# Hybrid decoder layer: q left unnormalised up to the exponential, both norm gains on k, masked copies for two heads

## Chip, cores and metric

One core of one Trainium2 chip. The metric is the device time of one launch in microseconds (us); for the kernel before, three runs gave 1914.89, 1916.03 and 1916.34, median 1916.03. The profile is of one execution.

## The reference

One layer over a sequence of 2048 tokens of width 1024, float32. The attention part is what the change touches:

```python
h = rms_norm(x, attn_norm_g);  z = h @ w_in          # columns: q, k, v, and three conv groups
q = rms_norm(z[..., :512].reshape(b, s, 8, 64), q_norm_g)     # 8 heads of 64
k = rms_norm(z[..., 512:640].reshape(b, s, 2, 64), k_norm_g)  # 2 kv heads
v = z[..., 640:768].reshape(b, s, 2, 64)
# blocks of 128 queries see their own block of keys and the one before
sc = einsum('bnqhgd,bnkhd->bnhgqk', q, k) * 64 ** -0.5
sc = where(0 <= query - key < 128 and key >= 0, sc, -1e30)
p = softmax(concatenate([sc, sink], -1))[..., :-1]   # one learned sink for each head
y_attn = einsum('bnhgqk,bnkhd->bnqhgd', p, v)
x = x + concatenate([rms_norm(y_attn, attn_out_g), rms_norm(y_conv, conv_out_g)]) @ w_out
x = x + square(relu(rms_norm(x, mlp_norm_g) @ w_up)) @ w_down
```

## The kernel before

A product in float32 is made of three products of rounded parts: every operand is split into a high and a low part (ACT rounds the high part, DVE subtracts it to get the low one), and TensorE adds high x high, high x low and low x high into one PSUM bank (`mm3`, L278 to L280).

The mixer stage, which the change touches, goes through four chunks of 512 tokens, each of four blocks of 128 (blocks b0 to b15). After it come the two MLP stages, products of `w_up` (L1454) and of `w_down` (L1571), which the change does not touch.

In a chunk, `mixers` runs the attention of the blocks one after another and weaves other work of the chunk between its steps (`fill`): the three convolution products (`pc`, `px`, `pb`), the output projection (`pout`), the transposes of the next chunk's input (`pt_a`) and its q, k, v projection (`pz`). The attention of a block has these steps:

- `qk_norm`: ACT squares q and k (L679), DVE sums over each of the 10 heads (L681), GpSimd raises the mean to the power -0.5 (L192, L193) into `rq`, 128 x 10, of which there are two buffers. DVE multiplies q and k by it (L684) and then by the gains (L686, once for the 512 columns of q and once for the 128 of k), in place in `z`.
- `qk_transpose`: TensorE transposes q (L697) and k (L699) into PSUM; ACT and DVE split them into `qt` and `kw` (L702 to L709).
- `softmax`: for each of four pairs of heads TensorE makes the scores against both key blocks (L724), ACT copies the own block's scores to `sc` (L732), and DVE overwrites those later than the query with the scores of the block before (L735), one head at a time. In block 0 there is none before, and a constant -1e30 is written. Then DVE takes the maximum of each row, negated (L737), limits it by the sink (L738), ACT makes eight exponentials with that as bias, each with its row sum (L741), and one of the sinks (L746); DVE adds the sink to the sums, takes the reciprocal and multiplies (L747 to L749).
- `values`: TensorE transposes the probabilities (L760), ACT and DVE split them (L766, L767), GpSimd keeps the part that lies in the own block (L773, into `pp` tiles with three buffers), and TensorE multiplies with v (L812).

PSUM has eight banks: three with the tag `mm` for projections, four with the tag `at` for attention, and one, `tr`, for the transposes of inputs, all handed out in turn. A scheduler fixes the order on each engine when the kernel is built: by the program's order, by its own estimates of durations, and by the offsets of `PRIO` (through `ahead(i)`) and the counts of `FILL`. Both tables stay as they are. On the chip every engine then takes its instructions in that order and waits where a semaphore asks for it. Loads go out in order on SP.

At the start, g_qk holds the two gains, 64 columns each, for all partitions; the gain of q is multiplied by 64 ** -0.5 (L1104), and the sinks are negated into `nsink` (L1107).

Of the kernel before, what the change touches and what calls it, by code (L numbers as in the profile page):

```python
# [11 lines left out]
AF = mybir.ActivationFunctionType  # L12
ALU = mybir.AluOpType
# [3 lines left out]
P = 128  # L17
# [3 lines left out]
HEADS, KVH, DH = 8, 2, 64  # L21
# [14 lines left out]
NT = CH // P  # L36
# [68 lines left out]
def hymba_layer(  # L105
# [19 lines left out]
    nc = tc.nc  # L125
# [37 lines left out]
    def zrow(name):  # L163
# [13 lines left out]
    later = const.tile([P, P], I32, name="later")  # L177
    nc.gpsimd.memset(later, 1)
    nc.gpsimd.affine_select(
        later, later, pattern=[[1, P]], compare_op=ALU.is_gt, fill=0.0, base=0, channel_multiplier=-1  # L180
    )
    neg = const.tile([P, 1], F32, name="neg")
# [305 lines left out]
    g_qk = const.tile([P, 2, DH], F32, name="g_qk")  # L488
# [144 lines left out]
    with tc.tile_pool(name="first", bufs=1) as first:  # L633
        with tc.manual_schedule(engines={ET.PE, ET.Activation, ET.DVE, ET.Pool, ET.SP}):
            rs0_in = first_chunk(first)

    with tc.tile_pool(name="mix_small", bufs=1) as mix_small, tc.tile_pool(name="mix", bufs=1) as mix:
# [10 lines left out]
        def project_qkv(c, h, z):  # L648

            z += [zrow(f"z{c}_{t}") for t in range(NT)]  # L650
            both = [[by_k(w) for w in weights(None, c, f"q{half}")] for half in range(2)]
            w4 = [w.rearrange("p (k c) -> p k c", k=KD) for w in weights(None, c, "qkv2")]

            for pc, t in ((0, 0), (0, 1), (1, 0), (0, 2), (0, 3), (1, 1), (1, 2), (1, 3)):
                n = 256 if pc else AW
                ps = bank("mm", f"pz{c}_{pc}_{t}")[:, :n]
                hk = lambda s, k, t=t: h[s][:, k, t * P : (t + 1) * P]
                wk = (lambda s, k: w4[s][:, k, :]) if pc else (lambda s, k: both[k // (KD // 2)][s][:, k % (KD // 2), :])
                for k in range(KD):
                    mm3(ps, lambda s, k=k: hk(s, k), lambda s, k=k: wk(s, k), k == 0, k == KD - 1)  # L660
                    if (k % 2 or not pc) and k < KD - 1:
                        yield
                nc.scalar.copy(z[t][:, pc * AW : pc * AW + n], ps)
                if pc and not t:
                    qk_norm(c * NT, z[0])
                yield


# [1 line left out]
            nc.gpsimd.memset(row("xt", f"xt_first{i}", 2)[:, :1], 0.0)  # L670

        nh = HEADS + KVH
        mix_small.tile([P, 8], F32, name="mix_pad")

        def qk_norm(b, zt):
            nm = f"b{b}"
            zqk = zt[:, : nh * DH].rearrange("p (h d) -> p h d", h=nh)
            sq = mix.tile([P, nh, DH], F32, tag="sq", name=f"sq_{nm}", bufs=1)
            nc.scalar.activation(sq, zqk, AF.Square, scale=DH**-0.5)  # L679
            ssq = mix_small.tile([P, nh], F32, tag="ssq", name=f"ssq_{nm}", bufs=2)  # L680
            nc.vector.tensor_reduce(ssq, sq, axis=AX.X, op=ALU.add)  # L681
            rq = mix_small.tile([P, nh], F32, tag="rq", name=f"rq_{nm}", bufs=2)
            rsqrt(rq, ssq)
            nc.vector.tensor_tensor(zqk, zqk, rq[:, :, None].to_broadcast([P, nh, DH]), op=ALU.mult)  # L684
            for i, (h0, h1) in enumerate(((0, HEADS), (HEADS, nh))):
                nc.vector.tensor_tensor(  # L686
                    zqk[:, h0:h1], zqk[:, h0:h1], g_qk[:, i, None, :].to_broadcast([P, h1 - h0, DH]), op=ALU.mult
                )
        def qk_transpose(b, zt):

            nm = f"b{b}"
# [17 lines left out]
                )  # L709
            return qt  # L710

        def softmax(b, qt):


            nm = f"b{b}"
            nk = (2 if b else 1) * P
            own = b % 2
            sc = mix.tile([P, HEADS, P], F32, tag="sc", name=f"sc_{nm}", bufs=2)
            for pr in range(HEADS // 2):
                kv = pr * 2 // GQ  # L720
                ps = bank("at", f"psc_{nm}_{pr}").rearrange("p (h s k) -> p h s k", h=2, s=2)
                for j in range(2):
                    for r in range(2):
                        nc.tensor.matmul(  # L724
                            ps[:, j].rearrange("p s k -> p (s k)")[:, :nk],
                            qt[:, pr, j, :],
                            kw[:, r, kv, :, :].rearrange("p s k -> p (s k)")[:, :nk],
                            start=r == 0,
                            stop=r == 1,
                        )  # L730
                s2 = sc[:, pr * 2 : pr * 2 + 2, :]
                nc.scalar.copy(s2, ps[:, :, own, :])  # L732
                for j in range(2):
                    other = ps[:, j, 1 - own, :] if b else neg.to_broadcast([P, P])
                    nc.vector.copy_predicated(s2[:, j, :], later, other)  # L735
            ngm = mix_small.tile([P, HEADS], F32, tag="ngm", name=f"ngm_{nm}", bufs=2)
            nc.vector.tensor_reduce(ngm, sc, axis=AX.X, op=ALU.max, negate=True)  # L737
            nc.vector.tensor_tensor(ngm, ngm, nsink, op=ALU.min)  # L738
            den = mix_small.tile([P, HEADS], F32, tag="den", name=f"den_{nm}", bufs=2)
            for hd in range(HEADS):  # L740
                nc.scalar.activation(  # L741
                    sc[:, hd, :], sc[:, hd, :], AF.Exp, bias=ngm[:, hd : hd + 1], accum_out=den[:, hd : hd + 1]
                )
            es = mix_small.tile([P, HEADS], F32, tag="es", name=f"es_{nm}", bufs=2)
            nc.vector.tensor_tensor(es, sink, ngm, op=ALU.add)
            nc.scalar.activation(es, es, AF.Exp)  # L746
            nc.vector.tensor_tensor(den, den, es, op=ALU.add)  # L747
            nc.vector.reciprocal(den, den)
            nc.vector.tensor_tensor(sc, sc, den[:, :, None].to_broadcast([P, HEADS, P]), op=ALU.mult)  # L749
            return sc  # L750
# [280 lines left out]
        def mixers(c, before, h, z):  # L1031


            last = c + 1 == NCHUNK
            n_fill = FILL[c]
            stage[0] = c
            at, yt, x1, h_next, z_next = [], [], [], [], []
            ra = small.tile([P, NT], F32, tag="ra", name=f"ra{c}", bufs=2)
            rc = small.tile([P, NT], F32, tag="rc", name=f"rc{c}", bufs=2)
            steps = besides(c, before, h, yt, rc, x1, h_next, z_next)  # L1040
            left = out_projection(c, 0, at, ra, x1)

            spare = (NT - 1) * NCT if last else 0

            def fill(n):
                nonlocal spare
                for _ in range(n):
                    if next(steps, steps) is steps and spare:
                        spare -= 1
                        next(left)  # L1050

            def scores(t):
                with ahead(0):
                    qt = qk_transpose(c * NT + t, z[t])
                fill(n_fill[t + 1][0])
                with ahead(1):
                    sc = softmax(c * NT + t, qt)
                if t + 1 < NT:
                    with ahead(2):
                        qk_norm(c * NT + t + 1, z[t + 1])  # L1060
                return sc

            if not c:
                qk_norm(0, z[0])
            fill(n_fill[0][0])
            sc = [scores(0)]
            fill(n_fill[0][1])
            for t in range(NT):
                b = c * NT + t
                if t + 1 < NT:  # L1070
                    sc.append(scores(t + 1))
                fill(n_fill[t + 1][1])
                for late in range(2):
                    if t and late == ((c, t) in LATE_RSTD):
                        with ahead(3):
                            attn_rstd(b - 1, sqa, ra[:, t - 1 : t])
                    if not late:
                        fill(n_fill[t + 1][2])
                a, sqa = values(b, z[t], z[t - 1][:, O_V:O_B] if t else v_last, sc[t], n_fill[t + 1][3:], fill)
                at.append(a)  # L1080
            for _ in steps:
                pass

            def rest():
                for i, _ in enumerate(left):
                    if i == REST:
                        attn_rstd(b, sqa, ra[:, NT - 1 : NT])
                    yield

            return rest(), h_next, z_next  # L1090

        z = z0
# [7 lines left out]
        for t in range(NT):  # L1100
            nc.tensor.transpose(pr[:, t * P : (t + 1) * P], rs0_at[:, 1, t * P : (t + 1) * P], ident)
        nc.scalar.copy(rs0_row, pr)
        with tc.issue_after(rs0_in):
            nc.gpsimd.tensor_scalar(g_qk[:, 0, :], g_qk[:, 0, :], DH**-0.5, None, op0=ALU.mult)  # L1104
        nsink = const.tile([P, HEADS], F32, name="nsink")
# [9 lines left out]
        for c in range(NCHUNK):  # L1115
            left, h, z = mixers(c, left, h, z)
# [215 lines left out]
    wts, ps, vs = {}, {}, {}  # L1332
# [278 lines left out]
```

## Time and profile before

| | before |
|---|---|
| median of three runs | 1916.03 us (1914.89 to 1916.34) |
| profiled execution: span from the first to the last instruction | 1913.4 us |
| instructions | 24557 |
| mean granted TensorE clock | 1.000 |

A time by the clock of the runs contains a little before and after the span: the median lies 2.6 us above it. In the rows below, a group's row gives the line, the engine, the operation, what it writes and reads with the shapes, and how often; then busy us in all and mean ns of one; then how long the engine was idle just before it, and who ended that. A row of the timeline begins with the start in us and the duration. "PEld" is TensorE's weight load, which runs ahead of the matmuls.

### The profile page before, as it was taken

The page shows a single profiled execution, that of the slowest core. Times are in us where ns is not written, and L with a number is a line of the kernel's source. Part 1 is how long each engine was busy: PE and PEld are TensorE (multiplying, and loading weights), DVE is VectorE, ACT ScalarE, POOL GpSimd, SP SyncE. Part 2 cuts the span into 40 slices and gives each one's busy share as a digit, 9 for nine tenths or more (in the row PEclk, how much of TensorE's full clock was granted, in tenths as well). Part 3 has the DMA queues.
Part 4 walks back from the last instruction along what each step waited for, and adds up shares of the span by engine and source line. Part 5 has one row for each costly group of instructions (what it writes and reads, how often), then busy time and mean ns, then how long its engine had stood idle before and what let it go on. Part 6 is the DMA issues. An engine that isn't in the chain of part 4 may idle for free.

```text
span 1913.4 us, 24557 instructions
## 1 busy us (share of the span) xinstructions
PE 1907.7 (100%) x8930; PEld 1591.1 (83%) x8930; DVE 1202.7 (63%) x1857; ACT 829.4 (43%) x1557; POOL 274.4 (14%) x477
## 2 busy tenths in 40 slices
PE   9999999999999999999999999999999999999999
PEld 8888888888888888888888888888888888888887
DVE  5895567448467759998788766666534334457531
ACT  6564245335445346544555545453332332232320
POOL 2123212302221112233101111111000000100000
PEclk9999999999999999999999999999999999999999
DMA  9984844564578688777576544448954457766631
GB/s 305 333 320 120 329 189 177 213 227 160 203 266 277 215 294 251 221 215 244 195 233 213 175 145 159 140 148 321 364 198 150 138 171 224 281 228 213 217 124 55
DMA packets 232792, 413.80 MB, mean 216 GB/s; under 512 B 51672, under 2 KB 136416, under 8 KB 219872
## 3 DMA queue, kind: packets, MB, share of 16 engines
q1 hardware_dynamic: 203840, 336.59, 52.0%
q0 software_dynamic: 15424, 51.40, 6.9%
q10 hardware_dynamic: 13408, 24.26, 3.4%
q8 instruction: 70, 1.15, 0.2%
q14 instruction: 50, 0.41, 0.1%
HBM read 286.35 MB, written 125.83 MB: 215 GB/s over the span
## 4 chain that ended last, share of the span: by engine, by line
PE 99%; DVE 0%; POOL 0%; issue 0%; ACT 0%; DVEq 0%; POOLq 0%
PE u L1454 32%; PE d L1571 32%; PE pout L278 3%; PE pout L280 3%; PE pout L279 3%; PE pz L278 2%; PE pz L280 2%; PE pz L279 2%; PE psc_b L724 2%; PE pb_c L280 2%; PE pb_c L279 2%; PE pb_c L278 2%; PE px_c L278 2%; PE px_c L279 2%; PE px_c L280 2%; PE po_b L812 1%
## 5 line engine op out<-in xcount | busy, mean ns | idle before, releaser
L1454 PE MATMUL u<-op_x,wop 128*128 128x512 f32 x2688 | 609.7, 389 | 0.0
L1571 PE MATMUL d<-op_w,op_f 128*128 128x512 f32 x2691 | 609.5, 389 | 0.0
L1571 PEld LDWEIGHTS d<-op_w,op_f 128*128 128x128 f32 x2691 | 504.8, 188 | 104.7
L1454 PEld LDWEIGHTS u<-op_x,wop 128*128 128x128 f32 x2688 | 504.3, 188 | 105.3 <-issue 0.3
L434 DVE TENSOR_TENSOR op_f<-op_f 128x1024 fp32r<-128x1024 f32 x112 | 136.8, 1224 | 235.6 <-ACT op_f L433 235.4
L433 ACT CAST op_f<-op_f 128x1024 fp32r<-128x1024 f32 x112 | 117.7, 1051 | 349.5 <-DMA op_f<-fop 349.0
L452 ACT CAST wop<-wu 128x512 fp32r<-128x512 f32 x156 | 96.1, 619 | 92.0 <-PE u L1454 88.3
L453 DVE TENSOR_TENSOR wop<-wu,wop 128x512 fp32r<-128x512 f32 x156 | 110.2, 708 | 31.8 <-ACT wop L452 16.7
L1190 POOL DMA_DIRECT2D fop<-s x96 | 52.1, 542 | 443.2 <-DVE s L1193 436.7
L1196 DVE TENSOR_TENSOR u<-u,u 128x512 f32<-128x512 f32 x128 | 87.7, 685 | 19.4 <-PE u L1454 19.2
L434 DVE TENSOR_TENSOR op_w<-raw,op_w 128x1024 fp32r<-128x1024 f32 x56 | 68.3, 1221 | 28.8 <-ACT op_w L433 28.8
L433 ACT CAST op_w<-raw 128x1024 fp32r<-128x1024 f32 x56 | 58.8, 1052 | 48.4 <-PE d L1571 26.3
L1202 ACT ACTIVATE u<-u 128x512 f32<-128x512 f32 x64 | 40.5, 632 | 56.5 <-DVE u L1196 54.3
L741 ACT ACTIVATE sc_b<-sc_b,ngm_b 128x128 f32<-128x128 f32 x128 | 49.7, 389 | 30.0 <-DVE ngm_b L738 30.0
L773 POOL TENSOR_SCALAR_AFFINE_SELECT pp_b<-pp_b 128x512 fp32r<-128x512 f32 x60 | 41.3, 701 | 134.6 <-ACT pp_b L766 66.1
L1403 POOL DMA_DIRECT2D wds<-raw x16 | 8.5, 533 | 329.9 <-DVE raw L1401 329.9
L453 DVE TENSOR_TENSOR wop<-wu_s,wop 128x512 fp32r<-128x512 f32 x64 | 45.9, 718 | 11.9 <-ACT wop L452 11.7
L452 ACT CAST wop<-wu_s 128x512 fp32r<-128x512 f32 x64 | 39.4, 620 | 29.3 <-PE u L1454 24.9
L278 PE MATMUL pout<-w_wo,yt_c 128*128 128x512 f32 x128 | 51.5, 402 | 0.0
L280 PE MATMUL pout<-w_wo,yt_c 128*128 128x512 f32 x128 | 51.0, 398 | 0.0
L279 PE MATMUL pout<-w_wo,yt_c 128*128 128x512 f32 x128 | 50.2, 393 | 0.0
L735 DVE COPY_PREDICATED sc_b<-later,psc_b 128x128 f32<-128x128 int32 x120 | 29.4, 296 | 32.0 <-ACT sc_b L732 31.7
(265 smaller groups left out, 3119.0 us busy)
## 6 DMA issues: line engine op xcount, KB each, us to landing
op_f<-fop SPq DMA_DIRECT2D x112, 512.0 KB, 4.3
raw<-in_w_down_dram SPq DMA_DIRECT2D x72, 512.0 KB, 4.1
wu<-in_w_up_dram SPq DMA_DIRECT2D x128, 256.0 KB, 3.8
w_wo<-wo SPq DMA_DIRECT2D x24, 1024.0 KB, 6.7
fop<-s POOLq DMA_DIRECT2D x96, 256.0 KB, 2.6
fop<-u ACTq DMA_DIRECT2D x64, 256.0 KB, 2.6
op_x<-xop SPq DMA_DIRECT2D x28, 512.0 KB, 6.0
w_q<-q SPq DMA_DIRECT2D x12, 1024.0 KB, 6.7
```

The source lines that it names most:

```text
L278: nc.tensor.matmul(ps, st(0), mv(0), start=first, stop=False)
L279: nc.tensor.matmul(ps, st(0), mv(1), start=False, stop=False)
L280: last_sum[0] = nc.tensor.matmul(ps, st(1), mv(0), start=False, stop=last).ins
L433: nc.scalar.copy(op[:, 0], raw)
L434: nc.vector.tensor_tensor(op[:, 1], raw, op[:, 0].bitcast(F32), op=ALU.subtract)
L452: splits.append(nc.scalar.copy(hi, blk).ins)
L453: lows.append(nc.vector.tensor_tensor(lo, blk, hi.bitcast(F32), op=ALU.subtract).ins)
L741: nc.scalar.activation(sc[:, hd, :], sc[:, hd, :], AF.Exp, bias=ngm[:, hd : hd + 1], accum_out=den[:, hd : hd + 1])
L1190: eng.dma_start(fop_dram[tb][ORDER_DOWN.index(i)][n // 2][:, n % 2], b)
L1196: return nc.vector.tensor_tensor(dst, ps, b, op=ALU.add).ins
L1454: nc.tensor.matmul(pt, wops[i][:, a, k, :], xops[tb, p][k // 2][:, b, k % 2, :], start=p not in GOES_ON and k + j == 0, stop=k + j == NB + ...
L1571: nc.tensor.matmul(ps[tb][j][:, cs], fs[tb][:, a, k, j * P : (j + 1) * P], w[:, b, k, cs], start=first and p not in GOES_ON and k + n == 0 ...
```

## The change

Four edits:

1. `qk_norm` multiplies only k by `rq` and by a gain; q stays as it comes from the projection. `rq` is returned and handed to `softmax` (through the table `rqs`).
2. The row maximum is taken of the scores without q's factor, so it is multiplied by `rq` of the head (a new DVE instruction of 128 x 8), and the exponential gets `rq` of the head as its scale, beside the bias that it has.
3. The gain of q is multiplied into that of k, once, on GpSimd, ahead of the factor 64 ** -0.5.
4. The masked copy takes a pair of heads in one instruction, with the mask repeated over the two heads.

```diff
-                    qk_norm(c * NT, z[0])
+                    rqs[c * NT] = qk_norm(c * NT, z[0])
...
             rsqrt(rq, ssq)
-            nc.vector.tensor_tensor(zqk, zqk, rq[:, :, None].to_broadcast([P, nh, DH]), op=ALU.mult)
-            for i, (h0, h1) in enumerate(((0, HEADS), (HEADS, nh))):
-                nc.vector.tensor_tensor(
-                    zqk[:, h0:h1], zqk[:, h0:h1], g_qk[:, i, None, :].to_broadcast([P, h1 - h0, DH]), op=ALU.mult
-                )
+            zk = zqk[:, HEADS:]
+            nc.vector.tensor_tensor(zk, zk, rq[:, HEADS:, None].to_broadcast([P, KVH, DH]), op=ALU.mult)
+            nc.vector.tensor_tensor(zk, zk, g_qk[:, 0, None, :].to_broadcast([P, KVH, DH]), op=ALU.mult)
+            return rq
+
...
-        def softmax(b, qt):
+        def softmax(b, qt, rq):
...
                 nc.scalar.copy(s2, ps[:, :, own, :])
-                for j in range(2):
-                    other = ps[:, j, 1 - own, :] if b else neg.to_broadcast([P, P])
-                    nc.vector.copy_predicated(s2[:, j, :], later, other)
+                other = ps[:, :, 1 - own, :] if b else neg[:, :, None].to_broadcast([P, 2, P])
+                nc.vector.copy_predicated(s2, later[:, None, :].to_broadcast([P, 2, P]), other)
...
             nc.vector.tensor_reduce(ngm, sc, axis=AX.X, op=ALU.max, negate=True)
+            nc.vector.tensor_tensor(ngm, ngm, rq[:, :HEADS], op=ALU.mult)
             nc.vector.tensor_tensor(ngm, ngm, nsink, op=ALU.min)
...
                 nc.scalar.activation(
-                    sc[:, hd, :], sc[:, hd, :], AF.Exp, bias=ngm[:, hd : hd + 1], accum_out=den[:, hd : hd + 1]
+                    sc[:, hd, :],
+                    sc[:, hd, :],
+                    AF.Exp,
+                    bias=ngm[:, hd : hd + 1],
+                    scale=rq[:, hd : hd + 1],
+                    accum_out=den[:, hd : hd + 1],
                 )
...
-                    sc = softmax(c * NT + t, qt)
+                    sc = softmax(c * NT + t, qt, rqs.pop(c * NT + t))
                 if t + 1 < NT:
                     with ahead(2):
-                        qk_norm(c * NT + t + 1, z[t + 1])
+                        rqs[c * NT + t + 1] = qk_norm(c * NT + t + 1, z[t + 1])
...
         with tc.issue_after(rs0_in):
+            nc.gpsimd.tensor_tensor(g_qk[:, 0, :], g_qk[:, 0, :], g_qk[:, 1, :], op=ALU.mult)
+        with tc.issue_after(rs0_in):
             nc.gpsimd.tensor_scalar(g_qk[:, 0, :], g_qk[:, 0, :], DH**-0.5, None, op0=ALU.mult)
```

Line numbers move by a few: in the changed kernel the masked copy is still L735, the two steps of the maximum are L738 and L739, the sum with the sink, the reciprocal and the normalisation are L753 to L755, the select is L779, and the three convolution lines L876, L879 and L881 are L882, L885 and L887.

The scheduler also places other rows anew, in the mixer stage alone. Two places matter for the prediction. The first is on DVE, around the softmax of block b4 in chunk 1 (z1_2 is the third block of that chunk, b6; psc_b5 are the scores of b5; y_c and pb_c belong to the convolution). Before:

```order
L737 TENSOR_REDUCE ngm_b4_2390<-sc_b4_2357 128x8
L876 TENSOR_TENSOR u_c1_0_1_2463<-px_c1_0_1_2521,u_c1_0_1_2463 128x512
L738 TENSOR_TENSOR ngm_b4_2390<-ngm_b4_2390,nsink_650 128x8
L879 TENSOR_SCALAR y_c1_0_1_2610<-u_c1_0_1_2463,cw_257 128x512
L745 TENSOR_TENSOR es_b4_2402<-sink_256,ngm_b4_2390 128x8
L881 SCALAR_TENSOR_TENSOR y_c1_0_1_2610<-u_c1_0_1_2463,cw_257,y_c1_0_1_2610 128x512 x2
L747 TENSOR_TENSOR den_b4_2393<-den_b4_2393,es_b4_2402 128x8
L748 RECIPROCAL den_b4_2393<-den_b4_2393 128x8
L749 TENSOR_TENSOR sc_b4_2357<-sc_b4_2357,den_b4_2393 128x1024
L895 TENSOR_TENSOR y_c1_0_0_2517<-pb_c1_0_0_2618,y_c1_0_0_2517 128x512
L899 TENSOR_TENSOR yt_c1_0_0_2644<-y_c1_0_0_2517,yt_c1_0_0_2644 128x512
L735 COPY_PREDICATED sc_b5_2528<-later_227,psc_b5_0_2529 128x128 x2
```

The same place in the changed kernel:

```order
L738 TENSOR_TENSOR ngm_b4_2370<-ngm_b4_2370,rq_b4_1937 128x8
L885 TENSOR_SCALAR y_c1_0_1_2586<-u_c1_0_1_2443,cw_257 128x512
L739 TENSOR_TENSOR ngm_b4_2370<-ngm_b4_2370,nsink_651 128x8
L887 SCALAR_TENSOR_TENSOR y_c1_0_1_2586<-u_c1_0_1_2443,cw_257,y_c1_0_1_2586 128x512
L751 TENSOR_TENSOR es_b4_2383<-sink_256,ngm_b4_2370 128x8
L887 SCALAR_TENSOR_TENSOR y_c1_0_1_2586<-u_c1_0_1_2443,cw_257,y_c1_0_1_2586 128x512
L901 TENSOR_TENSOR y_c1_0_0_2497<-pb_c1_0_0_2594,y_c1_0_0_2497 128x512
L753 TENSOR_TENSOR den_b4_2374<-den_b4_2374,es_b4_2383 128x8
L686 TENSOR_TENSOR z1_2_1789<-z1_2_1789,rq_b6_2560 128x128
L754 RECIPROCAL den_b4_2374<-den_b4_2374 128x8
L687 TENSOR_TENSOR z1_2_1789<-z1_2_1789,g_qk_255 128x128
L755 TENSOR_TENSOR sc_b4_2341<-sc_b4_2341,den_b4_2374 128x1024
```

The k multiply of b6 (L686, which reads `rq` of b6) now stands between the denominator and the reciprocal of b4, and the row L901 (L895 before) has gone ahead of both; behind L755 follow the split of y (L905) and the masked copies of b5. The multiplies of b6 stood far ahead of this place before.

The second place is GpSimd's queue in the same chunk; pp_b4 are the probabilities of b4. Before:

```order
L877 COPY halo_652<-u_c1_0_0_2436 128x2
L877 COPY halo_652<-u_c1_0_1_2463 128x2
L875 COPY u_c1_1_0_2739<-halo_652 128x2
L773 AFFINE_SELECT pp_b4_0_1_2714<-pp_b4_0_0_2713 128x512 x2
L773 AFFINE_SELECT pp_b4_1_1_2725<-pp_b4_1_0_2724 128x512 x2
```

In the changed kernel:

```order
L883 COPY halo_653<-u_c1_0_1_2443 128x2
L881 COPY u_c1_1_0_2715<-halo_653 128x2
L193 TENSOR_TENSOR rq_b6_2560<-ssq_b6_2558,mhalf_223 128x10
L779 AFFINE_SELECT pp_b4_0_1_2690<-pp_b4_0_0_2689 128x512 x2
L193 TENSOR_TENSOR rq_b7_2883<-ssq_b7_2881,mhalf_223 128x10
L779 AFFINE_SELECT pp_b4_1_1_2701<-pp_b4_1_0_2700 128x512 x2
```

The powers of b6 and b7, which stood far ahead of the halo copies before, now stand among the selects of b4, the one of b7 ahead of the select of b4's second half.

More of the change, by code (lines that the diff above doesn't have):

```diff
@@ L672, in hymba_layer @@
         nh = HEADS + KVH
+        rqs = {}
         mix_small.tile([P, 8], F32, name="mix_pad")
@@ L1056, in scores @@
                 with ahead(1):
-                    sc = softmax(c * NT + t, qt)
+                    sc = softmax(c * NT + t, qt, rqs.pop(c * NT + t))
                 if t + 1 < NT:
                     with ahead(2):
-                        qk_norm(c * NT + t + 1, z[t + 1])
+                        rqs[c * NT + t + 1] = qk_norm(c * NT + t + 1, z[t + 1])
                 return sc
             if not c:
-                qk_norm(0, z[0])
+                rqs[0] = qk_norm(0, z[0])
             fill(n_fill[0][0])
```

## The prediction

> **What bounds the kernel now.** I read the page first (engine shares, then the chain that ended last), then the stages, then what TensorE itself waited for.
>
> ```profile
> PE 1907.7 (100%) x8930; PEld 1591.1 (83%) x8930; DVE 1202.7 (63%) x1857; ACT 829.4 (43%) x1557; POOL 274.4 (14%) x477
> PE 99%; DVE 0%; POOL 0%; issue 0%; ACT 0%; DVEq 0%; POOLq 0%
> 30.00:690.60 660.60, 660.40 (x3418) 558.77 (x3417) 433.05 (x873) 307.23 (x813) 142.26 (x238) 1.00 0.64 234
> 690.60:1300.20 609.60, 609.60 (x2690) 504.33 (x2689) 478.99 (x696) 330.99 (x543) 103.75 (x168) 1.00 0.62 203
> 1300.20:1909.60 609.40, 609.33 (x2692) 504.47 (x2690) 277.59 (x269) 174.65 (x174) 22.72 (x44) 1.00 0.60 207
> 690.66 609.56 PE u L1454 x2688
> 249.10 0.87 PE ptp_b L760 x8
> ```
>
> The chain is TensorE from end to end. The three stage rows (stretch; busy PE, weight loads, DVE, ACT, POOL; clock; DMA) show it busy throughout at granted clock 1.00. The edited lines lie in the first stage, 30 to 690.6 us; what is issued in the two MLP stages stays as it was. The last two rows give TensorE's pace: 609.56 / 2688 = 0.227 us for a matmul of 512 columns, 0.87 / 8 = 0.109 us for a transpose. A busy PE is a modelled figure, so the test of "full" is whether TensorE waits. This is the view of waits for its weight loads, which go ahead of the matmuls and meet the semaphores first:
>
> ```profile
> PEld idle L579 <- POOL ident L172: 1.6, 1, 1.6
> PEld pt_a L306 <- DVE h_h L311: 0.9, 3, 0.5
> PEld pt_m L374 <- DVE xt_m L375: 0.7, 2, 0.5
> PEld pa_b L833 <- issue: 0.6, 2, 0.4
> PEld pout L278 <- DVE x L963: 0.6, 2, 0.3
> PEld pa_b L833 <- ACT yt_c L898: 0.5, 1, 0.5
> ...
> PEld ptq_b L697 <- ACT sc_b L732: 0.3, 1, 0.3
> ```
>
> In the mixer stage it waited for other engines 0.9 + 0.7 + 0.6 + 0.5 + 0.3 = 3.0 us in all, 2.2 of it for DVE. That is what lighter engines can give back.
>
> **The change part by part.** The sum is made against the profiled execution, span 1913.4 us; the median shown, 1916.0, lies 2.6 above it, and I keep those 2.6. TensorE executes the same matmuls, of the same shapes, so its own work changes by 0. What changes is the work of the others:
>
> ```profile
> L735 DVE COPY_PREDICATED sc_b<-later,psc_b 128x128 f32<-128x128 int32 x120 | 29.4, 296 | 32.0 <-ACT sc_b L732 31.7
> L684 DVE TENSOR_TENSOR z<-z,rq_b 128x640 f32<-128x640 f32 x16 | 14.5, 908 | 26.1 <-POOL rq_b L193 26.1
> L686 DVE TENSOR_TENSOR z<-z,g_qk 128x512 f32<-128x512 f32 x16 | 11.0, 687 | 0.2
> L686 DVE TENSOR_TENSOR z<-z,g_qk 128x128 f32<-128x128 f32 x16 | 4.5, 283 | 0.0
> L738 DVE TENSOR_TENSOR ngm_b<-ngm_b,nsink 128x8 f32<-128x8 f32 x16 | 2.6, 160 | 0.2
> L827 DVE TENSOR_TENSOR o_b<-o_b 128x256 f32<-128x256 f32 x16 | 6.7, 420 | 1.9 <-ACT o_b L826 1.8
> L828 DVE TENSOR_TENSOR o_b<-o_b 128x128 f32<-128x128 f32 x16 | 4.8, 300 | 0.2
> L741 ACT ACTIVATE sc_b<-sc_b,ngm_b 128x128 f32<-128x128 f32 x128 | 49.7, 389 | 30.0 <-DVE ngm_b L738 30.0
> L258 ACT ACTIVATE w_wo<-raw_wo,g_y 128x512 fp32r<-128x512 f32 x16 | 10.8, 720 | 0.0
> L255 ACT CAST w_wc<-raw_wc 128x512 fp32r<-128x512 f32 x8 | 4.4, 619 | 0.0
> L193 POOL TENSOR_TENSOR rq_b<-ssq_b,mhalf 128x10 f32<-128x10 f32 x16 | 33.3, 2080 | 1.3
> 29.66 0.60 POOL L1104 TENSOR_SCALAR g_qk<-g_qk 128x64 f32<-128x64 f32 x1
> 37.42 2.00 POOL L193 TENSOR_TENSOR rq_b<-ssq_b,mhalf 128x10 f32<-128x10 f32 x1
> ```
>
> *DVE.* The 640-wide multiply (L684) shrinks to 128 columns: 14.5 to 16 x 0.283 = 4.5 us, -10.0. The 512-wide gain multiply (L686) goes, -11.0; the 128-wide one stays. The extra multiply of the row maximum adds 16 x 0.160 = +2.6. No row shows a masked copy of 256 columns. Below, it costs no more than one of 128, 0.296; above, as much as two, 0.592; a step from 128 to 256 columns costs 0.420 - 0.300 = 0.120 (L828, L827), so I take 0.296 + 0.120 = 0.416. Two neighbours occupy about 29.4 / 60 = 0.49 us today, so 60 pairs give -4.4 (bounds -11.6 and +6.1). DVE is lighter by 10.0 + 11.0 + 4.4 - 2.6 = 22.8 us of its 433.
>
> *ACT.* An exponential that also reads a scale per row is in no row. Its bound below is 0; above, L258 (scale read per row, 720 ns) against L255 (none, 619): 0.101 us each, 0.8 for a block's eight, 12.9 for 128. I take the upper end, since those rows are the nearest. The exponential's row says 389 ns with its bias pointer. [...]
>
> *POOL.* One product of the two gains, bounded by 0 and by twice its neighbour L1104, 1.2 us, taken at 0.6, once, at 30 us. Its cover: the first user is the gain multiply of block 0's k, behind a power (L193) that begins at 37.42. On SP a few weight loads and stores change places around 117 to 150 us. Of those loads, the last two w_q go out at 135.5 and the first product that reads them starts at 150.7:
>
> ```profile
> w_q<-q SPq DMA_DIRECT2D x12, 1024.0 KB, 6.7
> 135.46 0.81 SPq L247 DMA_DIRECT2D w_q<-q  x2
> 150.68 0.48 PE L278 MATMUL pz<-w_q,h_h 128*128 128x512 f32 x1
> ```
>
> With 6.7 us to land that leaves 150.7 - 135.5 - 0.8 - 6.7 = 7.7 us; the rows move by less, so 0.
>
> *The added wait.* rq has two buffers, and the exponentials now read it: rq of block b+2 cannot be written before the exponentials of block b are done. The power is then done 2.08 us after them, and on DVE the k multiply stands between that block's denominator and its reciprocal, so the normalisation of the probabilities and the masked copies of the next block queue behind it; on POOL the causal selects queue behind the power. This holds for two blocks of every chunk, eight in all. The two places where least is left are both in chunk 1. First, block 4:
>
> ```profile
> 241.40 0.18 ACT L741 ACTIVATION_READ_ACCUMULATOR sc_b<-sc_b,ngm_b 128x1 f32 x1
> 241.92 0.20 DVE L748 RECIPROCAL den_b<-den_b 128x8 f32<-128x8 f32 x1
> 242.16 1.23 DVE L749 TENSOR_TENSOR sc_b<-sc_b,den_b 128x1024 f32<-128x1024 f32 x1
> 244.67 0.69 DVE L899 TENSOR_TENSOR yt_c<-y_c,yt_c 128x512 fp32r<-128x512 f32 x1 [0.69 <-ACT yt_c L898]
> 245.60 0.50 DVE L735 COPY_PREDICATED sc_b<-later,psc_b 128x128 f32<-128x128 int32 x2 [0.24 <-ACT sc_b L732]
> 248.94 1.03 PE L760 MATMUL ptp_b<-ident,sc_b 128*128 128x128 f32 x8
> 238.33 0.49 DVE L879 TENSOR_SCALAR y_c<-u_c,cw 128x512 f32<-128x512 f32 x1
> ```
>
> The exponentials end at 241.6. They will start some 0.6 later (the extra 0.16 and the 0.49 of L879, which is now between the two steps of the maximum) and last 0.8 longer: 243.0. Power done 245.1; k multiply, reciprocal, gain multiply, normalisation: 0.28 + 0.20 + 0.28 + 1.23 to 247.1; the split of y, 0.69, to 247.8; then the masked copy of block 5's first pair, 0.42, to 248.2. Its bank of the four "at" banks is the one into which TensorE transposes block 4 at 248.94. What is left is 0.7 us, 0.6 with a copy of 0.59, against 248.94 - 246.10 = 2.8 today. Cost 0.
>
> Second, the select of block 4's other half:
>
> ```profile
> 257.58 0.19 ACT L741 ACTIVATION_READ_ACCUMULATOR sc_b<-sc_b,ngm_b 128x1 f32 x1
> 259.81 1.22 POOL L773 TENSOR_SCALAR_AFFINE_SELECT pp_b<-pp_b 128x512 fp32r<-128x512 f32 x2 [7.83 <-PE po_b L812]
> 261.63 0.62 PE L812 MATMUL po_b<-pp_b,vd 128*128 128x512 f32 x2
> ```
>
> Block 5's exponentials end at 257.8, up to 258.6 with the scale; power to 260.7; two selects, 1.22, to 261.9. TensorE wants the first half at 261.63, when one select (0.6) is done at 261.3, and the second at 261.86. Cost 0 to 0.1, since the lighter DVE also starts these exponentials earlier.
>
> *Sum.* Gains: of the 2.2 us waited for DVE, 0 to 2.2; DVE is 5% lighter (22.8 of 433), but these are waits for a single eviction, which is as long as before, so I take 0.3. Losses: 0 to 0.1 at the second place, and a few tenths where transposes moved by some rows meet the one "tr" bank; I take 0.3. 1913.4 - 0.3 + 0.3 = 1913.4, and with the 2.6 **1916.0 us**.
>
> **The rivals.** *TensorE is not full after all.* [...] As a mechanism in rows: if the stage's pace were set by who feeds TensorE, the 22.8 us taken off DVE would come back in part; a quarter of it gives 1910.3. [...] Chance 0.03.
>
> *The waits for DVE vanish.* All 3.0 us go: 1913.0, which is still within 0.2%. It is inside the forecast's case, as is the case that the change doesn't do what it says and two heads' copy costs 0.59.
>
> *The new wait on rq takes the margin (slower).* Its place is block 4 and the first block of chunks 2 and 3, where the same rows follow one another. Price: the copy behind the k multiply comes 2.08 + 0.28 + 0.28 + 0.65 + 0.8 = 4.1 us later at most; where only 2.8 us are left, TensorE stops for 1.3; with the select as a fourth stop of that size 4 x 1.3 = 5.2, so 1921.2. It decides from the point where the masked copy of the next block's first pair ends after TensorE has reached the transposes. For it: 0.7 us is little, and it hangs on an exponential and a copy that no row shows. Against it: in block 4 the step-by-step sum above makes it 2.1, since the product of L895 now stands ahead of the wait, and in chunks 2 and 3 the next block's scores are not woven as closely into these transposes. Chance 0.12.
>
> **How the numbers follow.** Forecast 1916.0, 0.85. The rivals hold 0.12 (1921.2) and 0.03 (1910.3). 0.2% of 1916 is 3.8 us, about what a measurement of this kernel can tell from no change: 1912.2 to 1919.8. The range runs from 1913.0 (every wait gone) to 1919.9 (three stops of 1.3); beyond it lie most of both rivals, under 0.2. Faster 0.03, same 0.85, slower 0.12.
>
> **What would show it.** Right: TensorE's waits in the mixer stage again near 3 us, the MLP stages at 609 us, DVE's busy time in the stage near 410, and the exponential near 0.49 us. Wrong: a weight load of ptp or po waiting a microsecond or more for DVE or POOL in chunk 1 (slower rival), or the mixer stage shorter by more than 3 us (TensorE was not full). A longer power or exponential at block 4 by 0.7 us would be enough to begin the first.

## The result and the profile after

| | before | after |
|---|---|---|
| median | 1916.03 us (five runs, 1914.89 to 1918.32) | 1922.74 us (five runs, 1922.16 to 1923.60) |
| ratio | | 1.0036, 95% interval 1.0023 to 1.0048 |
| profiled execution, span | 1913.4 us | 1921.0 us |

The changed kernel is slower by 6.7 us. The forecast was 1916.0, with a range up to 1919.9. The spans differ by more, 7.6 us, since the profiled execution of the kernel before lies some 0.9 us below its median, if time and span are 1.7 us apart as they are for the change. First the page of the changed kernel: the engines' shares, the chain that ended last, and the two MLP groups.

```profile
span 1921.0 us, 24484 instructions
PE 1910.1 (99%) x8930; PEld 1592.0 (83%) x8930; DVE 1181.4 (62%) x1793; ACT 841.1 (44%) x1557; POOL 275.9 (14%) x478
PE 93%; DVE 2%; ACT 2%; DMA 1%; POOL 1%; issue 0%; SPq 0%; DVEq 0%; ACTq 0%; POOLq 0%
...
L1462 PE MATMUL u<-op_x,wop 128*128 128x512 f32 x2688 | 609.9, 389 | 0.1
L1579 PE MATMUL d<-op_w,op_f 128*128 128x512 f32 x2691 | 609.5, 389 | 0.0
```

TensorE's share of the chain fell from 99% to 93%, while its work and the two MLP groups stayed (609.7 and 609.5 before). So the loss lies in the mixer stage: the first product of the MLP starts at 697.89 us, where it started at 690.50. Next the groups of the edited lines, with shapes kept apart:

```profile
L742 ACT ACTIVATE sc_b<-sc_b,ngm_b,rq_b 128x128 f32<-128x128 f32 x128 | 61.5, 483 | 25.9 <-DVE ngm_b L739 25.9
L193 POOL TENSOR_TENSOR rq_b<-ssq_b,mhalf 128x10 f32<-128x10 f32 x16 | 33.4, 2087 | 39.9 <-ACT sc_b L742 39.3
L735 DVE COPY_PREDICATED sc_b<-later,psc_b 128x256 f32<-128x256 int32 x60 | 24.8, 443 | 27.2 <-ACT sc_b L733 26.9
L686 DVE TENSOR_TENSOR z<-z,rq_b 128x128 f32<-128x128 f32 x16 | 6.3, 394 | 26.5 <-POOL rq_b L193 26.5
```

The exponential takes 483 ns (389 before) and the copy of two heads 443 ns. The last field has the news: GpSimd now stands 39.3 us for the exponentials before the power L193, where it stood 1.3 us before the power in all. DVE stands 26.5 us for the power at the k multiply, in sum hardly more than the 26.1 us of L684 before. Most of this standing costs nothing: the whole loss is 6.7 us. What TensorE waits for tells where it does; this is the view of waits of its weight loads:

```profile
PEld pt_m L374 <- DVE xt_m L375: 4.4, 5, 3.2
PEld pt_a L306 <- issue: 2.3, 2, 1.6
...
PEld pt_a L306 <- DVE h_h L311: 1.3, 4, 0.4
PEld pa_b L839 <- issue: 0.9, 3, 0.4
PEld ptq_b L698 <- ACT sc_b L733: 0.9, 1, 0.9
...
PEld pa_b L839 <- ACT sc_b L733: 0.6, 1, 0.6
...
PEld po_b L818 <- POOL pp_b L779: 0.3, 1, 0.3
```

Two waits are new in size: 3.2 us for a transpose of the MLP's input (`pt_m`), and 1.6 us for one of the next chunk's input (`pt_a`).

**The stop at 584 us.** The timeline of the changed kernel (start, duration, engine and row), in chunk 3. The exponentials are those of b13, the power and the k multiply those of b15:

```profile
580.78 0.19 ACT L742 ACTIVATION_READ_ACCUMULATOR sc_b<-sc_b,ngm_b,rq_b 128x1 f32 x1
581.04 1.96 POOL L193 TENSOR_TENSOR rq_b<-ssq_b,mhalf 128x10 f32<-128x10 f32 x1 [3.00 <-ACT sc_b L742]
583.04 0.72 DVE L686 TENSOR_TENSOR z<-z,rq_b 128x128 f32<-128x128 f32 x1 [1.76 <-POOL rq_b L193]
...
584.00 1.22 DVE L755 TENSOR_TENSOR sc_b<-sc_b,den_b 128x1024 f32<-128x1024 f32 x1
585.14 1.28 DVE L773 TENSOR_TENSOR pp_b<-ptp_b,pp_b 128x512 fp32r<-128x512 f32 x2
586.34 0.68 DVE L375 TENSOR_TENSOR xt_m<-pt_m,g_cols 128x512 f32<-128x512 f32 x1
...
587.08 1.11 PE L374 MATMUL pt_m<-ident,xt_m 128*128 128x128 f32 x4 [2.79 <-DVE xt_m L375]
...
588.41 0.63 PE L279 MATMUL pb_c<-h_h,w_wb 128*128 128x512 f32 x1
588.84 0.63 PE L280 MATMUL pb_c<-h_h,w_wb 128*128 128x512 f32 x1
```

The power starts when the last exponential's row sum is read, and takes 1.96 us. DVE stands 1.76 us at the k multiply. Behind it in DVE's queue are b13's normalisation, the two splits of b12's transposed probabilities and, last, the eviction of a `pt_m` bank (L375). There is one bank with the tag `tr`, so TensorE's next `pt_m` transposes wait for that eviction. After the stop the matmuls start 0.43 us apart (588.41, 588.84), not 0.227. The windows of this stretch show why (busy PE, weight loads, DVE, ACT, POOL; then the granted clock):

```profile
578.00:583.00 5.00, 5.00 (x30) 4.26 (x29) 2.00 (x4) 4.14 (x17) 2.00 (x3) 1.00 0.79 261
...
588.00:590.00 2.00, 2.00 (x6) 1.61 (x6) 1.88 (x4) 1.15 (x1) 0.18 (x1) 0.50 0.45 165
```

The clock was 0.50. From 587.08 to 590.43 the four transposes and the six matmuls behind them took 3.35 us; the same ten took 1.83 us in the kernel before (579.51 to 581.34). That is 1.5 us more, beside 3.0 us without a matmul (584.12, when the next was due, to 587.08), so this place costs about 4.5 us.

**The stop at 136 us.** Here no power of rq is involved. The same view in chunk 0:

```profile
127.87 1.63 POOL L779 TENSOR_SCALAR_AFFINE_SELECT pp_b<-pp_b 128x512 fp32r<-128x512 f32 x2 [1.25 <-ACT w_wo L258]
128.00 0.95 PE L1015 MATMUL pc<-mean,ssc 128*128 128x1 f32 x8
...
130.22 1.04 POOL L193 TENSOR_TENSOR rc<-ms_c,mhalf 128x4 f32<-128x4 f32 x1
...
131.58 0.75 DVE L969 SCALAR_TENSOR_TENSOR x<-pout,rc,x 128x512 f32<-128x512 f32 x1 [1.54 <-POOL rc L1030]
...
136.79 0.69 DVE L311 TENSOR_TENSOR h_h<-pt_a,h_h 128x512 fp32r<-128x512 f32 x1
...
137.63 0.63 PE L306 MATMUL pt_a<-ident,xt_a 128*128 128x128 f32 x4 [1.21 <-DVE h_h L311]
```

And in the kernel before:

```profile
125.82 0.95 PE L1009 MATMUL pc<-mean,ssc 128*128 128x1 f32 x8
...
127.80 1.39 POOL L193 TENSOR_TENSOR rc<-ms_c,mhalf 128x4 f32<-128x4 f32 x1
...
129.41 1.23 POOL L773 TENSOR_SCALAR_AFFINE_SELECT pp_b<-pp_b 128x512 fp32r<-128x512 f32 x2
129.75 0.75 DVE L963 SCALAR_TENSOR_TENSOR x<-pout,rc,x 128x512 f32<-128x512 f32 x1
```

TensorE now makes the convolution's mean (`pc`) behind a block's products with v, at 128.00, and not ahead of them, at 125.82. Its norm factor `rc` comes from that mean through a power on GpSimd. Before, GpSimd took the power ahead of two selects; now the selects go first, but that is the smaller part: the power's input is ready 2.2 us later (129.15, not 126.97), and GpSimd takes it up 0.4 us after that. DVE's addition to x, which needs `rc`, begins at 131.58, not 129.75. The splits of q and k and the eviction of `pt_a` stand behind it, and TensorE waits. (The waits put this one down to "issue", the timeline to the eviction.)

### The profile page after: what moved, and what is told of

Its sections match the earlier page's. It is cut to its first block, busy times and chain, and to the rows that moved or that the text cites. A ratio compares the mean times of both kernels' runs of the same rounds, so it can differ in the third digit from the quotient of the medians.

```text
span 1921.0 us, 24484 instructions
## 1 busy us (share of the span) xinstructions
PE 1910.1 (99%) x8930; PEld 1592.0 (83%) x8930; DVE 1181.4 (62%) x1793; ACT 841.1 (44%) x1557; POOL 275.9 (14%) x478
## 4 chain that ended last, share of the span: by engine, by line
PE 93%; DVE 2%; ACT 2%; DMA 1%; POOL 1%; issue 0%; SPq 0%; DVEq 0%; ACTq 0%; POOLq 0%
PE u L1462 32%; PE d L1579 32%; PE pout L278 3%; PE pout L280 3%; PE pout L279 3%; PE pz L278 2%; PE pz L280 2%; PE pz L279 2%; PE po_b L818 1%; PE pb_c L280 1%; PE pb_c L278 1%; PE pb_c L279 1%; PE px_c L280 1%; PE px_c L278 1%; PE px_c L279 1%; PE pc_c L278 1%
## 5 line engine op out<-in xcount | busy, mean ns | idle before, releaser
L1462 PE MATMUL u<-op_x,wop 128*128 128x512 f32 x2688 | 609.9, 389 | 0.1
L1579 PE MATMUL d<-op_w,op_f 128*128 128x512 f32 x2691 | 609.5, 389 | 0.0
L742 ACT ACTIVATE sc_b<-sc_b,ngm_b,rq_b 128x128 f32<-128x128 f32 x128 | 61.5, 483 | 25.9 <-DVE ngm_b L739 25.9
L779 POOL TENSOR_SCALAR_AFFINE_SELECT pp_b<-pp_b 128x512 fp32r<-128x512 f32 x60 | 41.8, 708 | 127.6 <-ACT pp_b L772 69.8
L969 DVE SCALAR_TENSOR_TENSOR x<-pout,ra,x 128x512 f32<-128x512 f32 x32 | 24.0, 749 | 42.9 <-PE pout L280 40.9
```

The costliest lines, as they stand in the source:

```text
L742: nc.scalar.activation(sc[:, hd, :], sc[:, hd, :], AF.Exp, bias=ngm[:, hd : hd + 1], scale=rq[:, hd : hd + 1], accum_out=den[:, hd : hd + 1],)
L1462: nc.tensor.matmul(pt, wops[i][:, a, k, :], xops[tb, p][k // 2][:, b, k % 2, :], start=p not in GOES_ON and k + j == 0, stop=k + j == NB + ...
L1579: nc.tensor.matmul(ps[tb][j][:, cs], fs[tb][:, a, k, j * P : (j + 1) * P], w[:, b, k, cs], start=first and p not in GOES_ON and k + n == 0 ...
```

## The experiments

Three theories were set against each other. **W**: the new wait, rq of block b+2 for the exponentials of block b. **O**: the rearranged rows; the scheduler lays out the mixer stage anew for any edit, and the new order meets the chip's durations less well, wherever it does. **A**: the exponentials, 0.094 us longer each. All twelve runs, each timed beside the kernel before:

| run | median, us | ratio to before, 95% interval | profiled span |
|---|---|---|---|
| the change | 1922.74 | 1.0036 (1.0023 to 1.0048) | 1921.0 |
| rq4 | 1919.23 | 1.0013 (1.0004 to 1.0021) | 1917.8 |
| copies_only | 1918.25 | 1.0007 (0.9998 to 1.0016) | 1917.9 |
| norm_only | 1924.06 | 1.0040 (1.0028 to 1.0053) | 1925.7 |
| no_scale | 1923.32 | 1.0035 (1.0023 to 1.0048) | 1920.8 |
| wait_only | 1922.68 | 1.0028 (1.0017 to 1.0039) | 1919.0 |
| norm_rq4 | 1920.06 | 1.0019 (1.0010 to 1.0028) | 1917.0 |
| noscale_rq4 | 1919.77 | 1.0016 (1.0007 to 1.0025) | 1916.6 |
| order_only | 1919.19 | 1.0010 (1.0001 to 1.0019) | 1917.9 |
| norm_rq4_fill | 1919.11 | 1.0015 (1.0006 to 1.0024) | 1915.6 |
| rq4_fill | 1917.64 | 1.0008 (0.9999 to 1.0016) | 1914.3 |
| order_only2 | 1928.11 | 1.0061 (1.0049 to 1.0074) | 1926.4 |
| order_only3 | 1919.76 | 1.0019 (1.0010 to 1.0028) | 1915.4 |

The kernel before was timed again with each group of four: medians 1916.43 (the first four rows of runs), 1916.49 (the next four) and 1915.83 (the last four). Differences below are taken between ratios, times 1916.

### rq4: the change without the wait

```diff
-            rq = mix_small.tile([P, nh], F32, tag="rq", name=f"rq_{nm}", bufs=2)
+            rq = mix_small.tile([P, nh], F32, tag="rq", name=f"rq_{nm}", bufs=4)
```

> The changed kernel with four buffers for rq instead of two, so the power of block b+2 no longer waits for the exponentials of block b; TensorE's and ACT's instructions keep their order. Theory W (the added wait on rq makes the 3.2 us stop of TensorE at 584 us and the slow matmuls behind it): the stop at 584 us goes, 4 us come back, 1918.6 us. Theory O (the loss comes from the rearranged rows, wherever they are): the stop moves a little or stays, 1922 to 1923 us. Theory A (the exponentials are longer by 0.1 us each and the chain behind them is late): no gain either, 1922 to 1923 us. By all three the 1.4 us stop at 136 us, where no power of rq stands in the queues, stays.

Measured: 1.0013, so 0.0023 or 4.4 us came back. The orders of TensorE and ACT are those of the change, row for row; some 35 rows of DVE and 18 of GpSimd stand elsewhere. The stop at 584 us is gone, and the half clock with it: the mean granted clock is 0.999 in all five runs of the change and 1.000 in all eleven of rq4. The stop at 136 us stays, as all three theories had it, and two waits came up that the change did not have. The waits of rq4:

```profile
PEld pt_a L306 <- issue: 2.2, 2, 1.5
...
PEld psc_b L725 <- DVE qt_b L704: 1.1, 1, 1.1
PEld pt_m L374 <- DVE xt_m L375: 1.0, 3, 0.6
PEld psc_b L725 <- DVE kw L707: 0.9, 1, 0.9
```

The scores wait for the splits of q and k, which stand on DVE behind a subtraction in the MLP's input that waits for a store. In rq4's timeline:

```profile
592.22 0.69 DVE L388 TENSOR_TENSOR xt_m<-xt_m,xt_m 128x512 f32<-128x512 f32 x1 [2.41 <-DMA xop<-xt_m]
```

So W holds for its place, and something else is left: 0.0013, 2.5 us (0.8 to 4.0 by the interval).

### norm_only and norm_rq4: the same pair, with masked copies of one head

```diff
-                other = ps[:, :, 1 - own, :] if b else neg[:, :, None].to_broadcast([P, 2, P])
-                nc.vector.copy_predicated(s2, later[:, None, :].to_broadcast([P, 2, P]), other)
+                for j in range(2):
+                    other = ps[:, j, 1 - own, :] if b else neg.to_broadcast([P, P])
+                    nc.vector.copy_predicated(s2[:, j, :], later, other)
```

> The changed kernel with the masked copies of one head each, 296 ns, as before; the norm edits stay, rq has two buffers. Theory W: a stop of 2 to 4 us somewhere in the blocks whose rq waits for exponentials (b6, b7, b10, b11, b14, b15 and b2, b3), 1919 to 1924 us. Theory O: another order, so anything from 1915 to 1920 us, with stops where no rq stands. Theory A: as the changed kernel, 1921 to 1923 us.

> The norm edits with masked copies of one head each and four buffers for rq: against norm_only (1924.06 us) only the wait on rq goes. Theory W: the 3.7 us stop at 585 us goes with the slow matmuls behind it, 1918 to 1920 us. Theory O: 1920 to 1924 us, since the other stops stay and new ones can come. If what is left over the kernel before is 2 us or more, the longer exponentials or the rearranged rows make that.

Measured: 1.0040 with two buffers for rq and 1.0019 with four. The wait costs 0.0021, 4.0 us, here too. In norm_only TensorE waits 4.0 us for `pt_m` at 585 us, with matmuls at a granted clock of 0.50 behind (589 to 594 us); in norm_rq4 no wait for `pt_m` is over 0.5 us. norm_rq4 keeps the stop at 136 us.

### wait_only: the kernel before with nothing but the wait

```diff
             nc.scalar.activation(es, es, AF.Exp)
+            seen = mix_small.tile([P, HEADS], F32, tag="seen", name=f"seen_{nm}", bufs=2)
+            nc.scalar.activation(seen, es, AF.Copy, scale=rq[:, :1])
```

> The kernel before with nothing of the change but the wait: after the eight exponentials and that of the sinks ACT makes one copy of 128 x 8 that reads rq (0.19 us, sixteen in all), so the power of block b+2 must wait for block b's exponentials. Few other rows move on TensorE. Theory W (the wait on rq costs TensorE stops of some us in chunk 3 and near the other late powers): 1919 to 1924 us, with a stop of 2 us or more for pt_m near 575 to 585 us. Theory O (rearranged rows, wherever they are, make the loss): few rows are moved, so 1916 to 1917 us.

Measured: 1.0028, 5.4 us, at W's place. The timeline of wait_only:

```profile
581.56 1.96 POOL L193 TENSOR_TENSOR rq_b<-ssq_b,mhalf 128x10 f32<-128x10 f32 x1 [2.95 <-ACT seen_b L751]
583.56 1.25 DVE L685 TENSOR_TENSOR z<-z,rq_b 128x640 f32<-128x640 f32 x1 [0.71 <-POOL rq_b L193]
...
587.17 0.67 DVE L375 TENSOR_TENSOR xt_m<-pt_m,g_cols 128x512 f32<-128x512 f32 x1
```

The normalisation stands ahead of the power's user here, and still the splits and the `pt_m` eviction behind it end too late: TensorE stops 3.3 us. By the names in the two traces, fewer than 30 of TensorE's 8930 rows had changed places, and some 70 of DVE's 1857, so this is the wait and hardly the order. It also stops 1.0 us at a select near 263 us, the prediction's second place.

### no_scale and noscale_rq4: without the scale operand

```diff
                     bias=ngm[:, hd : hd + 1],
-                    scale=rq[:, hd : hd + 1],
                     accum_out=den[:, hd : hd + 1],
```

> The changed kernel with the scale left out of the exponentials (the output then lacks q's norm factor in the exponent): the exponentials take 389 ns again and do not read rq, so the added wait goes as well. Theory W: the stop at 584 us goes, 1915 to 1918.6 us. Theory A: the same, and the stop at 136 us goes too, 1914 to 1917 us. Theory O: rows rearranged once more, 1916 to 1922 us. This run measures the cost of the scale operand, expected 0.094 us each.

> Four buffers for rq and no scale in the exponentials (the output then lacks q's norm factor in the exponent): against rq4 (1919.23 us) only the 0.094 us of each exponential go, and some rows move. Theory A (the longer exponentials make the rest of the loss, at 136 us above all): 1916 to 1917 us, the stop at 136 us is 0.5 us or less. Theory O (the rest is the rearranged rows): 1918 to 1921 us, with a stop of over 1 us at 133 to 137 us as in no_scale.

My expectation of no_scale was wrong: it came out at 1.0035, like the change. I had taken the wait to go with the scale, but the product of the row maximum with rq reads rq too. The timeline of no_scale:

```profile
566.13 1.99 POOL L193 TENSOR_TENSOR rq_b<-ssq_b,mhalf 128x10 f32<-128x10 f32 x1 [5.97 <-DVE ngm_b L738]
...
568.15 0.29 DVE L686 TENSOR_TENSOR z<-z,rq_b 128x128 f32<-128x128 f32 x1 [1.91 <-POOL rq_b L193]
```

The power now waits for DVE (L738), and DVE for the power: it stands 1.91 us at once. With four buffers (noscale_rq4) this goes too, and 0.0019 or 3.6 us come back, a third pair for the price of the wait. Against rq4 only the exponentials differ, and the rows that move with them: 1.0016 against 1.0013. Shorter exponentials (389 ns) gave nothing that can be told, and the stop before `pt_a` is still there, 2.0 us at 132 us. So theory A is not borne out; a gain under some 2 us would lie within the intervals.

### copies_only: the masked copies alone

The kernel before with the `+` side of the fourth edit.

> The kernel before with only the masked copy taken for two heads at once; q is normalised as before. Theory W: no exponential reads rq, so no stop of a microsecond; DVE is 4 us lighter and the time is 1915 to 1917 us. Theory O: the scheduler sets the rows anew with this edit too, so stops of the size of the one at 136 us (1.4 us) can come up, 1917 to 1920 us. Theory A: 1915 to 1917 us, since the exponentials are as before (389 ns).

Measured: 1.0007, not told from no change. TensorE's waits grew all the same: 1.6 and 1.1 us for the splits of q and k near 594 us, behind a DVE that waits 3.08 us for the store, as in rq4. It is a place that neither rq nor the exponentials touch. But the store itself took 9.23 us to land there, and 6.08 in the kernel before, which the order of the rows alone doesn't explain.

### order_only, order_only2, order_only3: the same instructions in another order

One number of the table PRIO in the kernel before, in chunk 3 for order_only, in chunk 0 for order_only2, in chunk 1 for order_only3:

```diff
-    (200, 20, 180, 240, 0, 0, 40, 40, 240, 0, 0, 30, 0, 0),
+    (200, 40, 180, 240, 0, 0, 40, 40, 240, 0, 0, 30, 0, 0),
...
-    (60, 0, 160, -10, 30, 0, 20, -10, -20, 30, 0, 300, 0, 0),
+    (60, 10, 160, -10, 30, 0, 20, -10, -20, 30, 0, 300, 0, 0),
...
-    (220, -60, -60, -50, 40, 0, 20, 40, -60, 280, 0, 0, 0, 0),
+    (220, -40, -60, -50, 40, 0, 20, 40, -60, 280, 0, 0, 0, 0),
```

> The kernel before with the same instructions, of the same shapes, and one number of the table PRIO changed: the offset of softmax in chunk 3 is 40 instead of 20, which moves some 280 rows of TensorE and 85 of DVE, and no work. Theory O: 1917 to 1921 us, with stops of a microsecond in chunk 3 that the kernel before does not have. If the order hardly matters: 1916 to 1917 us, waits of 3 us in the mixer stage as before.

> The kernel before, its instructions unchanged, with the offset of softmax in chunk 0 at 10 instead of 0: some 200 rows of TensorE and 100 of DVE move. Theory O: 1917 to 1921 us, stops in chunk 0 or behind it. If order_only was one unlucky order: 1916 to 1917 us.

> The kernel before, its instructions unchanged, with the offset of softmax in chunk 1 at -40 instead of -60: some 315 rows of TensorE and 84 of DVE move. Theory O: 1917 to 1921 us, stops in chunk 1 or behind it. If order_only was one unlucky order: 1916 to 1917 us.

Measured: 1.0010, 1.0061 and 1.0019, that is 1.9, 11.7 and 3.6 us slower with no work changed; order_only2 lies far above what I expected. Its longest waits:

```profile
PEld pb_c L280 <- DVE w_wb L256: 6.2, 3, 3.5
PEld pt_a L306 <- issue: 2.5, 2, 1.6
PEld pt_a L306 <- DVE ms_b L835: 1.9, 1, 1.9
```

A product of the convolution waits for the split of its weights; that stands on DVE behind masked copies, which wait for ACT's score copies, and these stand on ACT behind the rounding of the same weights. ACT had itself stood 6.4 us for a store there, until 68.28 us (3.7 us until 59.04 in the kernel before). O holds: with no work changed, the three orders cost 2 to 12 us. In order_only the evidence is weakest: its interval begins at 1.0001, and its longest wait, 2.3 us near 590, is again behind a slow store (DVE stands 2.71 us for it).

### norm_rq4_fill and rq4_fill: the order mended at one place

Two numbers of the table FILL, for chunk 0, as in rq4_fill; norm_rq4_fill adds the two steps one place further on, (9, 6, 8, 10, 2), and takes off the same two:

```diff
-    ((14, 15), (9, 9, 11, 8, 1), (9, 6, 8, 8, 2), (10, 11, 9, 8, 4), (13, 10, 7, 6, 1)),
+    ((14, 15), (9, 9, 11, 8, 1), (9, 6, 10, 8, 2), (8, 11, 9, 8, 4), (13, 10, 7, 6, 1)),
```

> norm_rq4 with two numbers of FILL changed in chunk 0 (two steps of other work more before one block's values, two fewer before the next block's): TensorE makes the convolution's mean (pc) ahead of block 1's second product with v, so GpSimd takes the power of rc ahead of the second pair of selects, as in the kernel before. Theory O, at its place (in norm_rq4 rc comes 3.2 us later than in the kernel before, DVE stands for it, and pt_a with it at 132 to 147 us): the stop at 136 us goes, and 1.5 to 2.7 us come back, 1917.4 to 1918.6 us. If something else holds pt_a there (the longer exponentials): no change, 1920 us.

> rq4 (masked copies of two heads, four buffers for rq) with two numbers of FILL changed in chunk 0 to the same end. Theory O: the stop at 136 us goes, 1 to 2 us come back of 1919.23, so 1917.2 to 1918.2 us; the stops of 0.9 and 0.6 us at 593 to 596 us, where scores wait for DVE, stay. By no theory does it come below the kernel before (1916.4) by 0.2%, since TensorE has no more than 3 us of waits there to give.

Measured: rq4_fill 1.0008 (rq4: 1.0013), norm_rq4_fill 1.0015 (norm_rq4: 1.0019). The steps of 0.0005 and 0.0004 have the expected sign and are within the intervals; the traces are clearer. In rq4_fill the power of `rc` is back at 127.99 us, ahead of the two selects at 129.60 (in the change it comes at 130.22, behind two). In norm_rq4_fill `pc` gains little (its result is taken up at 128.27 us; in norm_rq4 it was done at 128.58), but a select that stood ahead of the power goes behind it, and the power comes at 129.02, not 131.41. TensorE's longest waits in the mixer stage of rq4_fill are:

```profile
PEld pt_a L306 <- DVE h_h L311: 1.4, 5, 0.4
PEld pt_m L374 <- DVE xt_m L375: 1.2, 4, 0.6
PEld pa_b L839 <- ACT sc_b L733: 0.6, 1, 0.6
```

No single wait is over 0.6 us, and the profiled span is 1914.3 us against 1913.4 before; that execution took 1916.05 us, 1.6 less than the median of the eleven. The median can't be told from the kernel before: by the interval it lies between 0.2 us below and 3 us above. So all four edits, without the wait and with the order mended at one place, come near the time of the kernel before, with DVE 20 us lighter, and not below it. No version tried beats the kernel before.

## Why the prediction was wrong

- **"TensorE's own work changes by 0", and lighter engines can give back 3 us at most**: right. The MLP groups stayed at 609.9 and 609.5 us, and rq4_fill, with DVE as light as in the change, gained nothing. So "TensorE is not full" is out.
- **The durations**: right. DVE's busy time over the whole mixer stage (30 to 690.6 us before, 30 to 697.9 after) fell from 433.1 to 412.1 us (22.8 predicted, 21.0 measured). The masked copy of two heads took 443 ns (416). The exponential took 483 ns, 94 more (101 predicted). That is off the path as far as noscale_rq4 can tell.
- **"The added wait ... Cost 0" is the step that failed first.** The mechanism was named rightly: power 2.08 us behind the exponentials, the k multiply ahead of the reciprocal. Wrong was "the two places where least is left are both in chunk 1". At block 4 there is no stop, as foretold, but the times of the sum are not those: the power begins at 245.24 us (243.0 foretold), the first pair's copy ends at about 249.9 (248.2), and the transposes begin at 251.59 (248.94), 2.6 us after the normalisation. All of the block came some 2 us later, so that room was left there is in part luck. The select of block 4's other half cost 0.3 us (0 to 0.1 predicted). But I measured the room of a block by its own probabilities. What the k multiply of b15 held up was other work in DVE's queue, the splits of the block before and the eviction of the only `tr` bank, to which TensorE comes back every 1.85 us (in the kernel before its `pt_m` transposes begin at 579.51, 581.34 and 583.19). rq4, norm_rq4, noscale_rq4 and wait_only price the wait at 4.4, 4.0, 3.6 and 5.4 us.
- **The slower rival** (1921.2, chance 0.12) had the mechanism, but not the place: not block 4 and the first blocks of chunks 2 and 3, but the second wait of chunk 3; and not four stops of 1.3 us but one of 3.0 and about 1.5 of slow matmuls behind it, which no rival had. That its 1921.2 lies near the 1922.7 measured is luck.
- **"A few tenths where transposes moved by some rows ...; I take 0.3"** is the term that was mis-sized. With the wait removed, 2.5 us of loss remain (rq4), and the three runs that change only the order lose 1.9 to 11.7 us. The stop of 1.6 us at 136 us is such a case: a mean went behind other products on TensorE, and a power behind two selects on GpSimd. I had read the order at places that rq touches, and not what else had moved on the queues of TensorE, DVE and GpSimd.
- The sum, by ratios: 6.9 us of loss (0.0036) are about 4.4 from the wait and 2.5 that stay without it, for which the order is the cause that the runs support; each is uncertain by 2 to 3 us as the intervals stand. At the profile's places, 4.5 us at 584 us and 2 us at 136 and 148 us carry most of it; the rest is waits of 0.3 to 0.9 us that these runs don't separate.
- **"What would show it"** looked for a wait of ptp or po in chunk 1. The right sign was in another row of the same view: any weight load that waits over a microsecond for DVE.

Left open: why the store that DVE waits for near 592 us lands later in rq4, copies_only and order_only than in the kernel before. In order_only it isn't sent out late: it goes out at 581.17 us, in the kernel before at 581.11, but it takes 8.84 us to land and not 6.08 (8.54 in rq4). What slows it wasn't tried, and with one profile of each kernel the traces don't tell whether it is so in every execution.

## What to carry to other kernels

An operand that is read later than before holds its buffer longer. With two buffers for rq this turned into a wait on the next writer (39.3 us of GpSimd's standing in all), and the price was set by what was queued behind that writer's user on DVE (the eviction of `pt_m`, about 4.5 us at 584 us), not by the data that the edit concerns; count buffers for each new reader (two readers here, as no_scale showed). In a kernel whose main engine is full, as here (3.0 us of waits in the mixer stage), 20 us of work taken off another were worth nothing that could be measured, while every rearrangement of a fitted order can cost (1.9, 11.7 and 3.6 us in the three runs that change only the order): time the same instructions in another order first, to know how large that effect is.

## What the hardware showed beside that

The granted clock fell to 0.50 behind some short stops. In the change a stop of 3.2 us was followed by matmuls at 0.43 us for about 3 us; in order_only a wait of 2.3 us (590.2 to 592.5) by a stretch at half clock:

```profile
590.00:592.00 2.00, 0.60 (x3) 0.17 (x1) 1.87 (x4) 0.58 (x2) 0.00 (x0) 1.00 0.41 159
592.00:593.50 1.50, 0.98 (x4) 0.77 (x5) 1.42 (x4) 1.21 (x4) 0.00 (x0) 0.95 1.00 354
593.50:596.20 2.70, 2.70 (x10) 2.38 (x10) 2.02 (x5) 1.12 (x4) 0.00 (x0) 0.50 0.05 16
```

In wait_only's profiled execution a stop of 3.3 us at the same point of the program was followed by full clock:

```profile
584.00:588.00 4.00, 1.13 (x6) 0.63 (x5) 4.00 (x7) 1.15 (x1) 1.15 (x2) 1.00 0.65 246
588.00:589.00 1.00, 1.00 (x7) 0.92 (x8) 0.96 (x3) 0.00 (x0) 0.43 (x1) 1.00 0.12 49
589.00:591.00 2.00, 2.00 (x12) 1.49 (x11) 2.00 (x4) 0.75 (x2) 1.37 (x3) 1.00 1.25 299
```

So the length of a stop alone does not tell whether the clock falls behind it: it fell to 0.50 behind 2.3 and 3.2 us and stayed at 1.00 behind 3.3. What decides was not shown; no run was made to test it. The other six executions of wait_only have a mean granted clock of 0.998 or 0.999 and took 0.7 to 2.9 us longer.
